# Three token blocks open the output accumulation, and VectorE takes the weight residues and the gate

## The chip, the cores and the metric

The kernel runs on one core of a Trainium2 chip. A core has TensorE (PE in the profile; its weight loads are PEld), VectorE (DVE), ScalarE (ACT), GpSimd (POOL) and SyncE (SP, which here issues all the DMAs). The metric is the device time of one execution in microseconds (us); lower is better.

## The reference, cut to what matters

One layer of sliding-window attention runs over 1024 tokens of width 2048. It has 32 query heads of size 64 and 4 key and value heads. The gate z is projected together with q, k and v.

```python
def swa_sink_mixer(h, w_in, sinks):               # h: (1, 1024, 2048)
    q, k, v, z = jnp.split(h @ w_in, [BRANCH, BRANCH + KV_A, BRANCH + 2 * KV_A], axis=-1)
...
    scores = jnp.einsum('bnqhgd,bnkhd->bnhgqk', q, kb) * (HEAD_DIM ** -0.5)
    scores = scores - slopes[:, :, None, None] * dist
    scores = jnp.where(valid[None, :, None, None], scores, NEG)
    p = jax.nn.softmax(jnp.concatenate([scores, sink_col], axis=-1), axis=-1)[..., :-1]
    o = jnp.einsum('bnhgqk,bnkhd->bnqhgd', p, vb).reshape(B, S, BRANCH)
    return o, z

    h = rmsnorm(x, g_pre)
    y = (o * jax.nn.silu(z)) @ w_out
    x = x + rmsnorm(y, g_post)
```

All inputs and outputs are float32.

## The kernel before, in words

**Products.** Every large matrix product is made in three passes. An operand is split into a part rounded for the matmul ("hi") and what is left of it ("lo"), and a product is hi·hi + lo·hi + hi·lo. A weight granule is 128x512. ACT casts its hi part (`g_hi`, L209), an elementwise engine subtracts to get its lo part (`g_lo`, L213), SP stores the lo part in DRAM (`lo`, L215), and in the second half it is loaded from there instead of made again. Of the granules of the input projection, those with `key[2] == 1` have their subtraction on GpSimd, 32 in all; the other subtractions are on VectorE.

**Stages.** The tokens go in two halves of 512. In each half come v, k, then eight quads of heads (`in_phase`), each of 16 slots of 12 matmuls: two accumulators for q and two for z. Between these matmuls stand those of the attention of the quad before: `s_ps` (scores), `o_ps` (values). After that the output projection runs over 16 k-tiles for each of four column chunks, with four accumulators, one for each block of 128 tokens.

**Spill.** The attention of the last quad has no further quad to stand between, so the first 13 k-tiles (`SPILL`) of output chunk 0 are spread among it. k-tile n of it is slot 128+n. Each k-tile takes 12 matmuls (`acc_o`): four token blocks, three passes. The lists `TSL_LAST` and `VSL_LAST` say in which slot the last quad's parts stand. The four accumulators of `acc_o` reuse the buffers of the last quad's `acc_i`; the fourth is freed when `z` has been read out of it (L510).

**Attention of a block.** `s_ps` is masked and gets its bias on DVE, goes through exp on ACT (`t`, L374), is scaled to `w` (L393), transposed to `wt` on DVE (L399) and rearranged to `px`. For most blocks `px` goes out to DRAM and back (`pd`, L408 and L411). For 36 blocks (those of the second half and the last quad's of the first) it is copied in 16 pieces by three engines; the string `MOVES` says which engine has which piece: A is ACT, D is DVE, P is GpSimd. Then come `f` hi (ACT, L421), `f` lo (DVE, L422), two masked selections `g` (GpSimd, L425), the value matmuls `o_ps` (L447), their copy `oc` and sum `s_o`, and the product with the gate, `u` (L463). That product is on GpSimd in the first half but for its last quad, else on VectorE. `u` is split in hi and lo for the output projection (`pump_parts`, L562 and L563), two parts ahead of their use (`LOOK_SPLIT`).

**Order.** The framework sets the order of each engine's instructions by a simulated timeline with its own costs. Matmuls are kept in the order of the program from slot 125 (`PIN_FROM`) to the end of the spill; elsewhere a ready matmul may be put ahead of one that is expected late. On one engine the instructions then run strictly in the order set.

Of the kernel before, what the change touches and what calls it, by code (L numbers as in the profile page):

```python
# [10 lines left out]
F32 = mybir.dt.float32  # L11
F32R = mybir.dt.float32r
# [4 lines left out]
ALU = mybir.AluOpType  # L17
AX = mybir.AxisListType

P = 128  # L20
# [3 lines left out]
NB = HALF // P  # L24
KC = D // P
# [10 lines left out]
NQUAD = NH // QUAD  # L36
# [7 lines left out]
LOOK_SPLIT = 2  # L44
LOOK_W = 3
# [5 lines left out]
W_BUFS = 3  # L51
PD_BUFS = 4
S_BUFS, O_BUFS = 3, 1
SPILL = 13
OUT_SLOT = 128 + SPILL
QSL, ZSL = ((4, 7), (8, 9)), (11, 15)
SSL, TSL, FSL, VSL = 8, 12, 16, (18, 15)
MOVES = "AADPAADPAADAAADP"
PRE_PARTS = (122, 124, 126)
PIN_FROM = 125  # L60
TSL_LAST, VSL_LAST = 14, ((18, 18, 18, 16), (18, 17, 16, 16))


@with_exitstack
def tile_swa_layer(
# [10 lines left out]
    nc = tc.nc  # L76
# [7 lines left out]
    hp = ctx.enter_context(tc.tile_pool(name="hp", bufs=1))  # L84
# [95 lines left out]
    wl = []  # L180
# [18 lines left out]
    def pump_split(limit):  # L199
        while state["split"] < min(limit, len(stream)):  # L200
            i = state["split"]
            pump_dma(i + 1)
            raw, lo = raws.pop(i)
            kind, key = stream[i][2:]
            if isinstance(kind, int):
                hi = wl[0][:, kind, :]
            else:
                hi = gp.tile([P, 512], F32R, tag="g_hi", name="g_hi", bufs=G_BUFS)
            nc.scalar.copy(hi, raw)  # L209
            if lo is None:  # L210
                lo = lo_tile()
                eng = nc.gpsimd if kind == "in" and key[2] == 1 else nc.vector
                eng.tensor_tensor(lo, raw, hi.bitcast(F32), op=ALU.subtract)  # L213
                kept[key] = dram.tile([P, 512], F32, name=f"lo{i}")
                nc.sync.dma_start(kept[key], lo.bitcast(F32))  # L215
            splits[i] = (hi, lo)
            state["split"] += 1

    def next_granule(look_split=LOOK_W, look_dma=LOOK_DMA):
        while isinstance(stream[state["use"]][2], int):  # L220
            state["use"] += 1
        i = state["use"]
        state["use"] += 1
        pump_split(i + 1 + look_split)
        pump_dma(i + 1 + look_dma)
        return splits.pop(i)
# [205 lines left out]
    def att_values(a, half, b):  # L432
        i = a["quad"]
        kv = i // 2
        pool = a["pool"]
        f, g = a.pop(("f", b))
        y = a["y"]
        o_ps = ps.tile([P, 4, 2, HD], F32, tag="o", name="o_ps", bufs=O_BUFS)
        flat = o_ps.rearrange("p a h i -> p (a h i)")
        for s in range(2):  # L440
            v = v_n[:, b + 1, kv, :] if s else v_s[:, b, kv, :]
            cols = slice(s * HD, (s + 1) * HD)
            terms = ((v, f[:, 0, :, cols]), (v, f[:, 1, :, cols]), (y[:, s, b, :], g[:, :, cols]))
            if half == 0 and b == 0:
                terms = terms[:2]
            for j, (lhsT, rhs) in enumerate(terms):
                ins = nc.tensor.matmul(  # L447
                    flat[:, s * 256 : (s + 1) * 256].rearrange("p (a i) -> p a i", i=HD), lhsT=lhsT, rhs=rhs,
                    start=s == 0 and j == 0, stop=j + 1 == len(terms), skip_group_check=True,
                )  # L450
                if s or j or state["pin"]:
                    tc.keep_in_program_order(ins)
        oc = pool.tile([P, 4, HD], F32, tag="oc", name="oc", bufs=1)
        s = pool.tile([P, 2, 2, HD], F32, tag="sb", name="s_o", bufs=1)
        s4 = s.rearrange("p s e i -> p (s e) i")
        nc.scalar.copy(oc[0:HD], o_ps[HD:P, :, 0, :])
        nc.scalar.copy(oc[HD:P], o_ps[0:HD, :, 1, :])
        nc.vector.tensor_tensor(s4[0:HD], o_ps[0:HD, :, 0, :], oc[0:HD], op=ALU.add)
        nc.vector.tensor_tensor(s4[HD:P], o_ps[HD:P, :, 1, :], oc[HD:P], op=ALU.add)
        sl = slice(b * P, (b + 1) * P)  # L460
        gate = nc.vector if half or i == NQUAD - 1 else nc.gpsimd
        for e in range(2):
            gate.tensor_tensor(  # L463
                a["u"][:, 2 * i + e, sl].rearrange("p (s i) -> p s i", i=HD),
                s[:, :, e, :],
                a["z", e][:, sl].rearrange("p (s i) -> p s i", i=HD),
                op=ALU.mult,
            )
# [6 lines left out]
    def run_events(slot):  # L475
        for fn in events.pop(slot, []):
            fn()
# [77 lines left out]
    def pump_parts(limit):  # L555
        while state["part"] < min(limit, len(parts)):
            i = state["part"]
            src, cols = parts[i]()
            hi = gp.tile([P, 512], F32R, tag="u_hi", name="u_hi", bufs=SPLIT_BUFS)
            lo = gp.tile([P, 512], F32R, tag="u_lo", name="u_lo", bufs=SPLIT_BUFS)  # L560
            hi_v, lo_v = (x.rearrange("p (k t) -> p k t", t=cols) if cols < 512 else x for x in (hi, lo))
            nc.scalar.copy(hi_v, src)  # L562
            nc.vector.tensor_tensor(lo_v, src, hi_v.bitcast(F32), op=ALU.subtract)  # L563
            pieces[i] = (hi, lo)
            state["part"] += 1

    def next_part():
        i = state["take"]
        state["take"] += 1
        pump_parts(i + 1 + LOOK_SPLIT)  # L570
        return pieces.pop(i)

    def out_slot(accs, k, fresh, done):
        gr = next_granule()
        u = next_part()
        for b in range(NB):
            for j, (w, uu) in enumerate(passes(gr, u)):
                mm(
                    accs[b],
                    lhsT=uu[:, b * P : (b + 1) * P],  # L580
                    rhs=w,
                    start=fresh and j == 0,
                    stop=done and j == 2,
                )

    def y_evac(acc, half, b, c, yg, gpost, junk):
        nc.scalar.activation(junk, acc, AF.Square, accum_out=ssp[:, half, b, c : c + 1])  # L587
# [49 lines left out]
    with tc.tile_pool(name="pro", bufs=1) as pro:  # L637
# [28 lines left out]
        for k in range(KC):  # L666
            if k % 2 == 0:
                gr = next_granule(1, 3)
# [29 lines left out]
    def out_accs(c):  # L698
        if c % 2 == 0:
            return [ps.tile([P, 512], F32, tag="acc", name="acc_o", bufs=4) for _ in range(NB)]  # L700
        tags = (("s", S_BUFS),) * S_BUFS + (("o", O_BUFS),) * O_BUFS
        return [ps.tile([P, 512], F32, tag=t, name="acc_s", bufs=n) for t, n in tags]
# [4 lines left out]
    with tc.tile_pool(name="att0", bufs=1) as att:  # L707
        def sq_load(b, c):
            xp = gp.tile([P, 512], F32, tag="raw", name="xp")
            nc.sync.dma_start(xp, xf[HALF + b * P : HALF + (b + 1) * P, c * 512 : (c + 1) * 512])  # L710
            at(SQ_SLOT + 6 * (4 * b + c) + 4, lambda: sq_make(xp, b, c))

        def sq_make(xp, b, c):
            xjunk = att.tile([P, 512], BF16, tag="oc", name="xjunk", bufs=1)
            tc.keep_in_program_order(nc.scalar.activation(xjunk, xp, AF.Square, accum_out=ssx1[:, b, c : c + 1]))

        for b in range(NB):
            for c in range(4):
                at(SQ_SLOT + 6 * (4 * b + c), lambda b=b, c=c: sq_load(b, c))
        at(SQ_SLOT + 6 * 16 + 4, lambda: x_scales(ssx1, rcol1))  # L720
        in_phase(0, h0, u0, att)
        accs = out_accs(0)
        for k in range(SPILL):
            run_events(128 + k)
            out_slot(accs, k, k == 0, False)
        state["pin"] = False
    h1 = (
        hp.tile([P, KC, HALF], F32R, tag="hh", name="h_hi1"),
# [2 lines left out]
    with tc.tile_pool(name="out0", bufs=1) as op:  # L731
# [26 lines left out]
        for c in range(4):  # L758
            if c:
                accs = out_accs(c)  # L760
# [13 lines left out]
    for k in range(KC):  # L774
        if k % 2 == 0:
            gr = next_granule()
# [10 lines left out]
    with tc.tile_pool(name="att1", bufs=1) as att:  # L787
        fins = {}

        def fin_start(b, c):  # L790
            fins[(b, c)] = finalize(att, b, c)

        for b in range(NB):
            at(2 * b, lambda b=b: y_scale(0, b))
            for c in range(4):
                s0 = FIN_SLOT + FIN_STEP * (4 * b + c)
                at(s0, lambda b=b, c=c: fin_start(b, c))
                at(s0 + 4, lambda b=b, c=c: fins.pop((b, c))())
        in_phase(1, h1, u1, att)
        accs = out_accs(0)  # L800
        for k in range(SPILL):
            run_events(128 + k)
            out_slot(accs, k, k == 0, False)
        state["pin"] = False
    assert not events, sorted(events)
    y01 = kvp.tile([P, 2, D], F32, tag="k", name="y01")
    yts = [y01[:, 0], y01[:, 1]] + [kvp.tile([P, D], F32, tag=t, name="y23") for t in ("vn", "vs")]
    wl += (
        hp.tile([P, KC, 512], F32R, tag="hh", name="wl_hi"),
        hp.tile([P, KC, 512], F32R, tag="hl", name="wl_lo"),  # L810
    )
    with tc.tile_pool(name="out1", bufs=1) as op:
        junk = op.tile([P, 512], BF16, name="junk2")
        for c in range(3):
# [65 lines left out]
```

## Time and profile before

| | |
|---|---|
| Median of 3 runs | 1275.71 us (1275.5 to 1277.07) |
| The profiled execution | 1278.27 us, of which the span 1276.6 us |
| PE busy | 1247.0 us, 98% of the span |
| DVE, ACT, POOL busy | 830.6, 783.2, 337.1 us (65%, 61%, 26%) |
| PE's chain of waits | 54% of the span is PE itself, 3% DMA, 1% each ACT, DVE and issue |

Times in the rows are from the span's start. A busy PE is not PE at its peak: the duration of a matmul overlaps the next one's, so the pitch from start to start is what it costs. In brackets stands the idle time ahead of an instruction and what ended it.

### The profile page before, as it was taken

Reading aid. Unit: us, or ns where it says so; the run is one execution under the profiler, and the core shown is the slowest. Engines: PE = TensorE matmul, PEld = TensorE weight load, DVE = VectorE, ACT = ScalarE, POOL = GpSimd, SP = SyncE. Lnnn points to the kernel's source line nnn. Section 1 sums busy time; section 2 is a strip of 40 time slices with the busy share of each in tenths; the row PEclk is TensorE's granted clock in tenths of the full one; section 3 lists DMA queues with packets and bytes.
Section 4 is the critical chain, followed back from the end, with each engine's and each line's share of the span. In section 5 each row is a group of like instructions: output and inputs, shape, how many; then the busy total and the mean of one; then the engine's idle time right before and its main releaser. Section 6 shows DMA issues by size and latency. Waiting matters only on the chain.

```text
span 1276.6 us, 20454 instructions
## 1 busy us (share of the span) xinstructions
PE 1247.0 (98%) x5889; PEld 1043.8 (82%) x5889; DVE 830.6 (65%) x2365; ACT 783.2 (61%) x2087; POOL 337.1 (26%) x549
## 2 busy tenths in 40 slices
PE   8989999999999989999999999999999999999997
PEld 8878888888887877888898888888888888877785
DVE  5636767667676688677732278787787777832344
ACT  4526767666666677555533377777767767854531
POOL 1332536536535532000003022242232232200000
PEclk9989999999999999999999999999999999999999
DMA  8556777767676755899886667667767676876625
GB/s 289 157 181 205 224 225 228 221 217 237 215 233 210 232 159 168 230 271 252 253 265 194 190 208 209 210 205 208 213 202 218 191 226 183 290 257 229 226 70 182
DMA packets 302576, 274.03 MB, mean 215 GB/s; under 512 B 51568, under 2 KB 213888, under 8 KB 302464
## 3 DMA queue, kind: packets, MB, share of 16 engines
q1 hardware_dynamic: 302464, 272.73, 70.0%
q8 instruction: 47, 0.77, 0.2%
q14 instruction: 65, 0.53, 0.2%
HBM read 198.21 MB, written 74.45 MB: 214 GB/s over the span
## 4 chain that ended last, share of the span: by engine, by line
PE 54%; DMA 3%; ACT 1%; issue 1%; DVE 1%; POOL 0%; DVEq 0%; POOLq 0%; ACTq 0%; SPq 0%
PE acc_i L318 28%; PE acc_o L318 10%; PE acc_s L318 7%; DMA raw<-in_w_out_a 3%; PE acc_l L843 3%; PE o_ps L447 2%; PE acc_v L617 2%; PE acc_k L318 2%; PE s_ps L318 1%; ACT u_hi L562 1%; ACT g_hi L209 0%; DVE y L855 0%; ACT junk L587 0%; DVE u_lo L563 0%; ACT wl_hi L209 0%
## 5 line engine op out<-in xcount | busy, mean ns | idle before, releaser
L318 PE MATMUL acc_i<-h_hi,g_hi 128*128 128x512 f32 x1024 | 401.3, 392 | 2.0 <-ACT g_hi L209 2.0
L318 PE MATMUL acc_i<-h_hi,g_lo 128*128 128x512 f32 x1024 | 401.0, 392 | 1.7 <-DVE g_lo L213 1.7
L318 PE MATMUL acc_i<-h_lo,g_hi 128*128 128x512 f32 x1024 | 400.7, 391 | 0.0
L209 ACT CAST g_hi<-raw 128x512 fp32r<-128x512 f32 x400 | 245.7, 614 | 123.8 <-PE acc_i L318 49.5
L318 PEld LDWEIGHTS acc_i<-h_hi,g_hi 128*128 128x128 f32 x1024 | 192.8, 188 | 41.2 <-ACT g_hi L209 2.4
L318 PEld LDWEIGHTS acc_i<-h_lo,g_hi 128*128 128x128 f32 x1024 | 193.0, 188 | 40.0
L318 PEld LDWEIGHTS acc_i<-h_hi,g_lo 128*128 128x128 f32 x1024 | 193.0, 189 | 34.0 <-DVE g_lo L213 2.0
L213 DVE TENSOR_TENSOR g_lo<-raw,g_hi 128x512 fp32r<-128x512 f32 x176 | 127.4, 724 | 62.0 <-ACT g_hi L209 60.0
L374 ACT ACTIVATE t<-t,m 128x129 f32<-128x129 f32 x256 | 102.6, 401 | 95.7 <-DVE m L364 93.9
L563 DVE TENSOR_TENSOR u_lo<-u,u_hi 128x512 fp32r<-128x512 f32 x128 | 88.9, 697 | 111.0 <-ACT u_hi L562 104.9
L425 POOL TENSOR_SCALAR_AFFINE_SELECT g<-f 64x512 fp32r<-64x512 f32 x112 | 99.8, 892 | 171.1 <-ACT f L421 135.3
L562 ACT CAST u_hi<-u 128x512 fp32r<-128x512 f32 x128 | 78.9, 618 | 84.9 <-PE acc_o L318 29.0
L405 ACT COPY px<-wt 32x128 f32<-32x128 f32 x324 | 96.3, 297 | 28.6 <-DVE wt L399 25.0
L318 PE MATMUL acc_o<-g_hi,u_hi 128*128 128x512 f32 x256 | 101.9, 398 | 4.6 <-DVE z L510 3.6
L318 PE MATMUL acc_o<-g_lo,u_hi 128*128 128x512 f32 x256 | 101.1, 395 | 0.0
L318 PE MATMUL acc_o<-g_hi,u_lo 128*128 128x512 f32 x256 | 100.5, 398 | 0.1
L364 DVE CUSTOM_DVE_ANT_0 t<-s_ps,t,nsink 128x128 f32<-128x128 f32 x256 | 87.9, 348 | 5.2
L345 POOL COPY t<-nsink 128x4 f32<-128x4 f32 x64 | 12.8, 203 | 277.4 <-DVE w L385 132.8
L144 POOL TENSOR_TENSOR rs_r<-rs_v,mhalf 128x1 f32<-128x1 f32 (+1 forms) x10 | 6.3, 645 | 297.0 <-DVE rs_v L142 297.0
L318 PE MATMUL s_ps<-k_x,q 128*128 128x320 f32 x256 | 76.6, 310 | 3.5 <-POOL q L503 3.5
L362 DVE COPY_PREDICATED s_ps<-mask,s_ps 128x64 f32<-128x64 uint32 x224 | 49.0, 223 | 46.0 <-PE s_ps L318 44.6
L422 DVE TENSOR_TENSOR f<-px,f 128x512 fp32r<-128x512 f32 x64 | 50.7, 793 | 41.6 <-ACT f L421 41.2
(150 smaller groups left out, 2179.3 us busy)
## 6 DMA issues: line engine op xcount, KB each, us to landing
raw<-in_w_in_a SPq DMA_DIRECT2D x288, 256.0 KB, 3.6
lo<-g_lo SPq DMA_DIRECT2D x208, 256.0 KB, 2.7
g_lo<-lo SPq DMA_DIRECT2D x192, 256.0 KB, 3.5
raw<-in_w_out_a SPq DMA_DIRECT2D x128, 256.0 KB, 4.0
pd<-wt SPq DMA_DIRECT2D x28, 256.0 KB, 2.2
px<-pd SPq DMA_DIRECT2D x112, 64.0 KB, 2.2
xp<-in_x SPq DMA_DIRECT2D x16, 256.0 KB, 3.9
xb<-in_x SPq DMA_DIRECT2D x64, 64.0 KB, 4.1
```

The source lines that it names most:

```text
L209: nc.scalar.copy(hi, raw)
L213: eng.tensor_tensor(lo, raw, hi.bitcast(F32), op=ALU.subtract)
L318: ins = nc.tensor.matmul(*args, **kw)
L362: nc.vector.copy_predicated(s3[:, :, P:], mask.unsqueeze(1).broadcast_to([P, 2, QTR]), s3[:, :, 0:QTR])
L364: nc.vector.tensor_tensor_reduce(out=t[:, 0:P], in0=s3[:, 0, QTR:], in1=t[:, 0:P], scale=1.0, scalar=nsink[:, i : i + 1], op0=ALU.add, op1 ...
L374: nc.scalar.activation(t, t, AF.Exp, bias=m, scale=-1.0, accum_out=den)
L405: copy(x[qrows[3 - k], c, :], wt[qrows[c], 3 - k, :])
L422: pin(nc.vector.tensor_tensor(f[:, 1], x, f[:, 0].bitcast(F32), op=ALU.subtract))
L425: nc.gpsimd.affine_select(out=g[dst].rearrange("p a (s i) -> p (a s) i", i=HD), in_=f[HD:P, l].rearrange("p a (s i) -> p (a s) i", i=HD).b ...
L562: nc.scalar.copy(hi_v, src)
L563: nc.vector.tensor_tensor(lo_v, src, hi_v.bitcast(F32), op=ALU.subtract)
L843: nc.tensor.matmul(acc, lhsT=uu[:, i * P : (i + 1) * P], rhs=w[:, k, :], start=k == 0 and j == 0, stop=k == KC - 1 and j == 2,)
```

## The change

In the spill of either half, the first two k-tiles are computed for token blocks 0 to 2, and only then for block 3. The spill has 14 k-tiles, not 13, and in the first half the values of the last block stand one slot later. In the spill the parts of `u` are split at most one ahead at first (`look`). In the first half the 32 GpSimd subtractions of weights and the GpSimd gate products are put on VectorE. In `MOVES` two of ACT's nine pieces go to GpSimd. The tile `wl` is allocated ahead of the second spill, since the longer spill looks ahead as far as its first granule.

```diff
-SPILL = 13
+SPILL = 14
...
-MOVES = "AADPAADPAADAAADP"
+MOVES = "AADPAADPAPDAPADP"
...
-TSL_LAST, VSL_LAST = 14, ((18, 18, 18, 16), (18, 17, 16, 16))
+TSL_LAST, VSL_LAST = 14, ((18, 18, 18, 17), (18, 17, 16, 16))
...
-                eng = nc.gpsimd if kind == "in" and key[2] == 1 else nc.vector
-                eng.tensor_tensor(lo, raw, hi.bitcast(F32), op=ALU.subtract)
+                nc.vector.tensor_tensor(lo, raw, hi.bitcast(F32), op=ALU.subtract)
...
-        gate = nc.vector if half or i == NQUAD - 1 else nc.gpsimd
         for e in range(2):
-            gate.tensor_tensor(
+            nc.vector.tensor_tensor(
...
+    def spill(accs):
+        run_events(128)
+        first = next_granule(LOOK_W - 1), next_part(1)
+        out_mms(accs, range(3), *first, True, False)
+        run_events(129)
+        second = next_granule(LOOK_W - 1), next_part(1)
+        out_mms(accs, range(3), *second, False, False)
+        out_mms(accs, (3,), *first, True, False)
+        out_mms(accs, (3,), *second, False, False)
+        for k in range(2, SPILL):
+            run_events(128 + k)
+            out_slot(accs, k, False, False, min(LOOK_SPLIT, 13 - k) if k < SPILL - 1 else LOOK_SPLIT)
...
         accs = out_accs(0)
-        for k in range(SPILL):
-            run_events(128 + k)
-            out_slot(accs, k, k == 0, False)
+        spill(accs)
```

The change also moves instructions on engines whose own lines it does not touch. First TensorE at the start of the first quad: `acc_i_799` is the quad's first accumulator, `acc_i_880` its second, and `g_hi_744` and `g_lo_746` are the two halves of the last granule of the first one. Before:

```order
L318 MATMUL acc_i_799<-h_hi0_128,g_hi_744 128x512
L318 MATMUL acc_i_880<-h_hi0_128,g_hi_820 128x512
L318 MATMUL acc_i_880<-h_hi0_128,g_lo_822 128x512
L318 MATMUL acc_i_880<-h_lo0_129,g_hi_820 128x512
L318 MATMUL acc_i_880<-h_hi0_128,g_hi_820 128x512
```

Now:

```order
L317 MATMUL acc_i_799<-h_hi0_128,g_hi_744 128x512
L317 MATMUL acc_i_799<-h_hi0_128,g_lo_746 128x512
L317 MATMUL acc_i_799<-h_lo0_129,g_hi_744 128x512
L317 MATMUL acc_i_799<-h_hi0_128,g_hi_744 128x512
L317 MATMUL acc_i_799<-h_hi0_128,g_lo_746 128x512
```

Before, the twelve matmuls of granule 820 stood behind the first matmul of granule 744; now the twelve of 744 stand together, and 820 comes 24 matmuls behind them. The queue of SP at the same place, before (lo17 is the store of `g_lo_746`):

```order
L215 DMA lo18_768<-g_lo_766 128x512
L191 DMA raw_806<-in_w_in_a 128x4x128
L215 DMA lo19_804<-g_lo_802 128x512
L191 DMA raw_826<-in_w_in_a 128x4x128
L215 DMA lo20_824<-g_lo_822 128x512
L191 DMA raw_846<-in_w_in_a 128x4x128
L215 DMA lo17_748<-g_lo_746 128x512
```

Now:

```order
L214 DMA lo17_748<-g_lo_746 128x512
L191 DMA raw_806<-in_w_in_a 128x4x128
L214 DMA lo18_768<-g_lo_766 128x512
L191 DMA raw_826<-in_w_in_a 128x4x128
L214 DMA lo19_804<-g_lo_802 128x512
L191 DMA raw_846<-in_w_in_a 128x4x128
```

The load of `raw_806` stood behind the store of `g_lo_766`; it now stands behind that of `g_lo_746`, which is made earlier. The third place is ACT in the first spill, where `u_hi_5890` before and `u_hi_5886` now are the same part of `u`, number 3 counted from 0 (`th` belongs to the gate z, `w` to the next block's probabilities). Before, part 2 and part 3 have these places:

```order
L562 CAST u_hi_5813<-u0_794 128x512
L374 ACTIVATE t_5770,den_5772<-t_5770,m_5771 128x129
L209 CAST g_hi_5805<-raw_5740 128x512
L393 ACTIVATE w_5844<-t_5622,rec_5842 128x3x32 x2
L393 ACTIVATE w_5844<-t_5622,rec_5842 128x32 x2
L393 ACTIVATE w_5844<-t_5622,rec_5842 128x4x32 x2
L562 CAST u_hi_5890<-u0_794 128x512
```

Now:

```order
L510 ACTIVATE th_5755<-z_5754 128x512
L373 ACTIVATE t_5622,den_5624<-t_5622,m_5623 128x129
L373 ACTIVATE t_5770,den_5772<-t_5770,m_5771 128x129
L392 ACTIVATE w_5834<-t_5622,rec_5832 128x3x32 x2
L392 ACTIVATE w_5834<-t_5622,rec_5832 128x32 x2
L392 ACTIVATE w_5834<-t_5622,rec_5832 128x4x32 x2
L373 ACTIVATE t_5770,den_5772<-t_5770,m_5771 128x129
L560 CAST u_hi_5886<-u0_794 128x512
```

The split that stood between `th` and the six `w` instructions now stands behind these and one more exp.

## Rows read from the trace of the kernel before

**Rows 1.** What PE waited for: in total, how often, the longest.

```profile
PE acc_o L318 <- DVE z L510: 3.6, 1, 3.6
PE s_ps L318 <- POOL q L503: 3.5, 3, 1.6
...
PE o_ps L447 <- POOL g L425: 1.6, 2, 1.0
PE o_ps L447 <- ACT f L421: 1.4, 1, 1.4
...
PE o_ps L447 <- DVE f L422: 1.0, 1, 1.0
```

**Rows 2.** A piece of the chain of waits in the output projection: start, length, what, how many.

```profile
521.03 43.52 PE acc_s L318 x192
```

**Rows 3.** The timeline of PE, SP, POOL and DVE in turn at the start of the first quad: start, duration, engine, line, what.

```profile
67.53 0.50 PE L318 MATMUL acc_i<-h_hi,g_hi 128*128 128x512 f32 x1 [1.99 <-ACT g_hi L209]
69.75 0.79 PE L318 MATMUL acc_i<-h_hi,g_lo 128*128 128x512 f32 x1 [1.72 <-DVE g_lo L213]
...
72.05 0.63 PE L318 MATMUL acc_i<-h_hi,g_hi 128*128 128x512 f32 x1
72.47 0.63 PE L318 MATMUL acc_i<-h_hi,g_lo 128*128 128x512 f32 x1
...
56.07 0.39 SPq L191 DMA_DIRECT2D raw<-in_w_in_a  x1
64.40 0.34 SPq L215 DMA_DIRECT2D lo<-g_lo  x1
...
59.39 1.48 POOL L213 TENSOR_TENSOR g_lo<-raw,g_hi 128x512 fp32r<-128x512 f32 x1
...
57.32 0.69 DVE L301 TENSOR_TENSOR k<-acc_k,rrow 128x512 f32<-128x512 f32 x1 [1.71 <-ACT rrow L264]
```

**Rows 4.** Three stretches at a lower clock: stretch, its length, PE, PEld, DVE, ACT and POOL busy (instructions), the clock granted to PE as a share of full speed, DMA share, GB/s.

```profile
68.20:74.90 6.70, 5.15 (x12) 4.09 (x13) 1.85 (x4) 0.05 (x1) 0.00 (x0) 0.50 0.64 193
467.60:470.90 3.30, 3.30 (x10) 2.62 (x9) 3.29 (x12) 2.75 (x10) 0.00 (x0) 0.50 0.52 141
505.10:511.80 6.70, 6.06 (x16) 4.80 (x17) 2.68 (x7) 1.35 (x3) 1.05 (x1) 0.50 0.51 172
```

**Rows 5.** The timeline at the start of the first spill: PE, DVE, ACT, and DVE again.

```profile
466.91 0.50 PE L318 MATMUL acc_o<-g_hi,u_hi 128*128 128x512 f32 x1 [3.64 <-DVE z L510]
...
466.16 0.69 DVE L510 TENSOR_TENSOR z<-acc_i,rrow 128x512 f32<-128x512 f32 x1
...
469.97 1.65 ACT L393 ACTIVATE w<-t,rec 128x96 f32<-128x96 f32 x6
...
471.65 0.71 DVE L399 STREAM_TRANSPOSE wt<-w 128x512 f32<-128x512 f32 x1 [0.59 <-ACT w L393]
```

**Rows 6.** The timeline at the end of the first spill: ACT, DVE, POOL, PE.

```profile
499.36 2.77 ACT L405 COPY px<-wt 32x128 f32<-32x128 f32 x9
...
503.20 0.61 ACT L421 CAST f<-px 128x512 fp32r<-128x512 f32 x1
...
509.58 0.62 ACT L562 CAST u_hi<-u 128x512 fp32r<-128x512 f32 x1 [1.25 <-DVE u L463]
...
498.86 1.11 DVE L405 COPY px<-wt 32x128 f32<-32x128 f32 x4
...
504.01 1.14 DVE L422 TENSOR_TENSOR f<-px,f 128x512 fp32r<-128x512 f32 x1
505.07 0.68 DVE L213 TENSOR_TENSOR g_lo<-raw,g_hi 128x512 fp32r<-128x512 f32 x1
...
503.88 0.74 POOL L425 TENSOR_SCALAR_AFFINE_SELECT g<-f 64x512 fp32r<-64x512 f32 x1 [4.21 <-ACT f L421]
505.22 1.05 POOL L425 TENSOR_SCALAR_AFFINE_SELECT g<-f 64x512 fp32r<-64x512 f32 x1 [0.61 <-DVE f L422]
...
506.33 0.58 PE L447 MATMUL o_ps<-g,v_y 128*128 128x256 f32 x1 [0.54 <-POOL g L425]
```

**Rows 7.** The timeline ahead of the longest wait of `s_ps`, at 395 us: ACT, SP, POOL.

```profile
391.72 0.62 ACT L421 CAST f<-px 128x512 fp32r<-128x512 f32 x1 [2.41 <-DMA px<-pd]
...
388.30 1.74 SPq L411 DMA_DIRECT2D px<-pd  x4
...
392.47 1.12 POOL L425 TENSOR_SCALAR_AFFINE_SELECT g<-f 64x512 fp32r<-64x512 f32 x1 [3.94 <-issue]
```

**Rows 8.** Groups of instructions: busy time, mean ns of one, idle time before. The first is of the stretch 62 to 461 us (the first half's quads), the second and third of the whole run, the last of 652 to 1085 us (the second half up to its spill).

```profile
L213 DVE TENSOR_TENSOR g_lo<-raw,g_hi 128x512 fp32r<-128x512 f32 x97 | 73.2, 754 | 47.3 <-ACT g_hi L209 45.6 <-DMA lo<-g_lo 1.2
...
L213 POOL TENSOR_TENSOR g_lo<-raw,g_hi 128x512 fp32r<-128x512 f32 x32 | 41.5, 1298 | 29.9 <-ACT g_hi L209 14.4 <-DMA raw<-in_w_in_a 12.2 <-DMA lo<-g_lo 2.0
...
L463 POOL TENSOR_TENSOR u<-s_o,z 128x128 f32<-128x128 f32 x56 | 25.2, 471 | 45.7 <-DVE s_o L459 45.7
...
L463 DVE TENSOR_TENSOR u<-s_o,z 128x128 f32<-128x128 f32 x56 | 16.5, 335 | 0.3
```

**Rows 9.** Busy time by stretch, columns as in rows 4: a stretch of the first half's quads, the second half's quads, its spill.

```profile
280.00:330.00 50.00, 48.99 (x232) 41.04 (x231) 36.92 (x111) 34.82 (x104) 31.36 (x41) 1.00 0.75 228
...
697.00:1085.00 388.00, 388.00 (x1824) 325.40 (x1823) 285.86 (x983) 274.39 (x797) 98.58 (x196) 1.00 0.69 205
1085.00:1121.00 36.00, 36.00 (x172) 30.22 (x171) 28.65 (x90) 28.76 (x78) 8.43 (x16) 1.00 0.84 287
```

More of the change, by code (lines that the diff above doesn't have):

```diff
@@ L565, in pump_parts, with next_part, out_mms @@
             state["part"] += 1
-    def next_part():
+    def next_part(look=LOOK_SPLIT):
         i = state["take"]
         state["take"] += 1
-        pump_parts(i + 1 + LOOK_SPLIT)
+        pump_parts(i + 1 + look)
         return pieces.pop(i)
[L573 to L576, printed above, removed]
+    def out_mms(accs, blocks, gr, u, fresh, done):
+        for b in blocks:
             for j, (w, uu) in enumerate(passes(gr, u)):
@@ L584, in out_slot @@
                 )
+    def out_slot(accs, k, fresh, done, look=LOOK_SPLIT):
+        out_mms(accs, range(NB), next_granule(), next_part(look), fresh, done)
+    def spill(accs):
[10 more added lines that the diff above has]
+            out_slot(accs, k, False, False, min(LOOK_SPLIT, 13 - k) if k < SPILL - 1 else LOOK_SPLIT)
     def y_evac(acc, half, b, c, yg, gpost, junk):
@@ L799, in tile_swa_layer @@
         in_phase(1, h1, u1, att)
+        wl += (
+            hp.tile([P, KC, 512], F32R, tag="hh", name="wl_hi"),
+            hp.tile([P, KC, 512], F32R, tag="hl", name="wl_lo"),
+        )
         accs = out_accs(0)
-        for k in range(SPILL):
-            run_events(128 + k)
-            out_slot(accs, k, k == 0, False)
+        spill(accs)
         state["pin"] = False
@@ L807, in tile_swa_layer @@
     yts = [y01[:, 0], y01[:, 1]] + [kvp.tile([P, D], F32, tag=t, name="y23") for t in ("vn", "vs")]
[L808 to L811, printed above, removed]
     with tc.tile_pool(name="out1", bufs=1) as op:
```

## The prediction

> **What bounds the kernel now.** I read the page first (the table above): PE is busy nearly all the time, so a gain can only come from the places where PE stands still or runs at the low clock. The list of PE's waits comes next [rows 1]: the reader is to see that they are few and single, a wait for z, three for q, some around `o_ps`. What a matmul costs at full speed is read from the output projection: 43.52 us for 192 is 0.227 us each [rows 2]. Then the granted clock by stretch [rows 4]: at three places it is 0.50, the lower level of 1.2 GHz, and each lies right behind a wait. There a matmul costs 72.47 - 72.05 = 0.42 us [rows 3], so a wait is paid for twice. Four places remain:
>
> - A, start of the first quad. PE stops at 67.53 - 1.99 = 65.54 and the low clock ends at 74.90 [rows 3, 4]. In these 9.36 us run 13 matmuls (the one at 67.53 and the twelve of rows 4's first line), worth 13 x 0.227 = 2.95. Lost: 6.4 us.
> - B, start of the spill. 3.64 idle for z [rows 5], then 3.30 us at the low clock, of which 1 - 0.227/0.42 = 46% is lost, 1.5 [rows 4]. Lost: 5.1.
> - C, the last block's values. 1.4 for f hi, 1.0 for f lo, 0.54 for g [rows 1, 6], then 6.06 busy us at the low clock, 46% of it 2.8 [rows 4]. Lost: 5.7.
> - D, inside the first half's quads: 3.5 for q and a part of the 1.6 for g [rows 1], some 4.5 us; the clock is 1.00 in the stretch of [rows 9] that has 1.0 of it.
>
> **The change part by part.**
>
> *Weight subtractions, at A.* The POOL subtraction of 59.39 was over at 60.87, long before PE wanted it [rows 3]. PE waits because of the order: it takes granule 820 ahead of 746's residue, and 820 is late, since SP's queue had its load behind the store lo18, and nothing was issued from 56.07 until 64.40 [rows 3]. In the new order PE keeps to granule 744, whose residue DVE makes right behind the k read-out (57.32 + 0.69 = 58.0, then about 0.75 by the mean of [rows 8]): 58.8 against a want at 65.5. The load behind lo17 leaves some 5 us earlier than 64.40. Granule 820 is now wanted behind 744's twelve matmuls and 24 more, at 65.5 + 36 x 0.227 = 73.7, while before it was there by 69.75 with its load late. The granules between hang on DVE's k work, whose last residue before came in time for 69.75. I see nothing late: **-6.4**. The bounds are -6.4 and 0 (the wait goes to one of the granules between).
>
> *Weight subtractions and gates, at D.* DVE gets 32 x 0.754 = 24.1 and 56 x 0.335 = 18.8 us [rows 8], 42.9 us over the 399 us of the first half's quads, 5.4 in 50; its fullest stretch goes from 36.92 to 42.3 of 50, 85% [rows 9]. PE does not wait for DVE there, but for q and g of POOL. POOL itself was idle 3.94 before g: f came late on ACT, which waited for the px loads, issued at 388.30 [rows 7]. So a lighter POOL does not take these waits away, and a fuller DVE moves that chain (w, transposition, f, q) back a little. In the second half DVE is at 285.86 of 388, 74%, with the gates on it, and PE is busy through all 388 [rows 9]. Bounds: -2 (the POOL pieces in the chain, 0.47 and 1.30 each, no longer in the way at some of four places) and +4 (each of the four longer by a subtraction and a gate, about 1 us). I take **+0.5**, near no change, since the order on ACT and POOL around f, g and q stays.
>
> *Block order, at B.* Nine more matmuls stand ahead of the fourth block: PE gets to it at 466.91 - 3.64 + 9 x 0.227 = 465.3. z, ahead of which DVE waits for ACT's copies, starts about when it did: two ACT copies less, 2 x 2.77/9 = 0.6 earlier [rows 6], and two gates more, 2 x 0.335 = 0.7 later [rows 8]. So PE waits until 467, 1.7 instead of 3.64: -1.9. A stretch of the quads with 50.00 - 48.99 = 1.0 us idle kept the clock at 1.00 [rows 9], while 3.64 in one piece lost it, so I take the low clock as gone too, though 1.7 lies between: -1.5. Against it stands part 3 of u. Its split is asked for later, and on ACT it now stands behind the six w and one more exp. With the two instructions gone that stood before w (0.6 each, a cast of u and a cast of a granule), w starts at 468.8 to 469.5 in place of 469.97 [rows 5], the hi part is there after 1.65 + 0.4 + 0.6, at 471.5 to 472.2, and the lo part behind the transposition, 0.71 [rows 5], and four copies, 1.1 [rows 6], at about 473.5. PE wants them 18 matmuls (4.1) and two scores (0.3) behind 467, at 471.4, the lo part 0.5 later. A new wait of about 1.7, and the low clock after it in a third of cases, 0.5. Sum **-1.2**; bounds -5.1 (no wait left) and +1.7 (the new wait 3.4, with the low clock).
>
> *One more k-tile, at C.* Twelve matmuls, 2.7 us, stand ahead of the values, out of what came behind. The f cast at 503.20 stood behind nine copies, a cast of u and one of a granule [rows 6]; two copies (0.6) and the granule's cast (0.6) are out of its way. The three waits come to 2.9 us, and the k-tile and the shorter chain take 2.7 + 1.2 off, which would leave nothing; but the chain goes on through DVE and POOL, and an earlier PE start (A, B) does not bring it forward. I leave 1.1 of a wait with the clock up: **-4.6**; bounds -5.7 and -2 (1.5 of wait, and half of the low clock stays). Behind the values only twelve matmuls, 2.7 us, now cover the path to the next part of u: its hi part ended at 510.20, 3.9 behind the last release of PE at 506.33 [rows 6], of which four value matmuls at half clock took about 1.2. That leaves 2.7 against 2.7, and the first matmuls use only the hi part, so it holds by a hair.
>
> POOL and DVE hinder each other there. The f subtraction beside POOL's selection took 1.14, beginning 0.13 behind it; the second selection took 1.05 where the first had 0.74, beside a subtraction of a granule begun at 505.07 [rows 6]. In the Trainium skill, "SBUF — State Buffer", section "Who interferes with whom", a VectorE instruction with two SBUF inputs and a GpSimd instruction that reads SBUF shut each other out for the whole of one of them; the trace agrees (503.88 + 0.74 = 504.62, and the subtraction ends 0.53 later). In the new order no granule's subtraction stands ahead of f's, which would then start first and hold POOL: by the rule the second selection ends some 0.4 earlier, and C would be -5.0. I leave it out of the sum.
>
> *MOVES and wl.* In the second spill PE waits for nothing, 36.00 busy of 36 [rows 9], and ACT has 7.2 us idle there. Nothing to gain; two more POOL copies cost little beside POOL's 8.43 of 36: 0, bounds -1 and +2.
>
> Sum: -6.4 + 0.5 - 1.2 - 4.6 = -11.7 us. The profiled execution took 1278.27, so it would be 1266.6; the median of the runs is 2.56 lower, and I put the same sum on it: 1275.71 - 11.7 = **1264.0 us**.
>
> **The rivals.**
>
> 1. *All spill waits go.* z starts earlier than I put it and part 3 is in time. For it: DVE loses waits of ACT there. Against it: the order behind w. -6.4 - 5.1 - 5.7 = -17.2, 1258.5.
> 2. *The waits move.* Part 3 stops PE as long as z did, with the low clock, and C keeps half of its own: B 0, C -2.8, -6.4 + 0.5 - 2.8 = -8.7, 1267.0. For it: the clock fell at all three places where waits came together [rows 4].
> 3. *VectorE becomes the bound in the first half, and the kernel is slower.* Each of the 28 blocks there has a chain with a DRAM round trip, and at four or more of them it is already on the edge [rows 1, 7]. A subtraction (0.75) and half a pair of gates (0.33) ahead of w's transposition or of f move it by 1.1 us. If half the blocks show it, 14 x 1.1 = 15.4 us is more than A to C give (12.2): 1279. It decides from 12.2 / 14 = 0.87 us a block. Against it: PE waits nowhere for DVE there, and the second half runs without a wait. In the Trainium skill, "Perfetto Trace Analysis", section "Optimizing Scalar/DVE Operations", work may go from a saturated VectorE to other engines, even GpSimd; the change goes the other way, but no stretch shows DVE saturated (85% by the sum above).
> 4. *The order is not what decides at A*: the wait stays, behind another granule, -5.3, 1270.4.
>
> **How the numbers follow.** The forecast has 0.52 (its own range 1261 to 1267), rival 1 0.14, rival 2 0.19, rival 4 0.09, rival 3 0.06. About 0.2% (2.6 us) can be told from no change. Faster by more than that are all but rival 3 and a tenth of rivals 2 and 4 with D at its upper bound: 0.90; same 0.05; slower 0.05. The range goes from 1256 (rival 1 with some of D) to 1271 (rival 4).
>
> **What would show it.** Right: no wait of `acc_i` in the first 30 us of the first quad and a clock of 1.00 there; a wait for z below 2 us; a wait of `acc_o` for u_hi or u_lo in the k-tile behind it; a short wait at the values with the clock up. Wrong: SP still silent from 56 to 64 us; new waits of `acc_i`, `s_ps` or `o_ps` for DVE between 100 and 460 us; the low clock behind part 3.

## The result, and the profile after

| | before | changed |
|---|---|---|
| median | 1275.61 us (1274.31 to 1277.07, 4 runs) | 1265.49 us (1264.41 to 1266.23, 4 runs) |
| ratio to before | | 0.992, 95% interval 0.9903 to 0.9937 |
| profiled execution, span | 1278.27, 1276.6 us | 1265.93, 1264.2 us |

The forecast was 1264.0 us, 11.7 less; measured are 10.1 less. To see where they come from, I take for every matmul the distance to the next one's start, less the pitch of its size at full clock (0.227 us for 512 columns, 0.146 for 320, 0.117 for 256), and sum what is left by place. This counts waits and low clock together.

| lost, us | prologue | A | D | B | C | second half | its end | sum |
|---|---|---|---|---|---|---|---|---|
| before | 7.3 | 6.7 | 8.0 | 5.7 | 6.6 | 3.3 | 4.9 | 42.5 |
| changed | 5.6 | 0.1 | 8.8 | 5.4 | 1.6 | 3.5 | 5.2 | 30.2 |

The sums differ by 12.3 us, as do the spans (12.4). I do not put the prologue's 1.7 us down to the change: over the profiles below it lies between 4.5 and 6.0 us whatever the kernel. In this pair of profiles the gain is A and C, 11.6 us; B and D give nothing.

The list of PE's waits of the changed kernel, its head, as in [rows 1]:

```profile
PE o_ps L446 <- POOL g L424: 3.9, 5, 1.3
PE s_ps L317 <- DVE m L363: 2.2, 1, 2.2
...
PE acc_o L317 <- DVE u_lo L561: 0.9, 1, 0.9
...
PE s_ps L317 <- POOL q L501: 0.7, 2, 0.4
PE o_ps L446 <- DVE f L421: 0.5, 2, 0.3
```

The wait for z, longest before, is gone from the list. A wait for m stands in its place, a new one for u_lo has come, and what was a wait for q is now one for g. Two stretches by windows (columns as in [rows 4]): the first quad's start, and the one low-clock stretch that is left.

```profile
458.60:462.00 3.40, 3.40 (x9) 2.64 (x8) 3.37 (x10) 1.15 (x3) 0.00 (x0) 0.50 0.43 130
62.40:80.00 17.60, 17.60 (x79) 14.59 (x78) 11.16 (x17) 5.68 (x10) 5.31 (x6) 1.00 0.69 217
```

At A, PE is busy throughout with the clock at 1.00. The other rows at A, of SP and DVE, against [rows 3]:

```profile
57.41 0.39 SPq L191 DMA_DIRECT2D raw<-in_w_in_a  x1
62.93 0.34 SPq L214 DMA_DIRECT2D lo<-g_lo  x1
...
68.87 0.69 DVE L212 TENSOR_TENSOR g_lo<-raw,g_hi 128x512 fp32r<-128x512 f32 x1
```

SP is still silent for 5.5 us, and the lo half of granule 820 (the last row) is done at 69.56. Before it was made here (ACT, DVE):

```profile
65.58 1.26 ACT L308 CAST k_x<-k 64x512 fp32r<-64x512 f32 x2 [2.28 <-DVE k L301]
66.86 0.62 ACT L209 CAST g_hi<-raw 128x512 fp32r<-128x512 f32 x1
...
69.00 0.69 DVE L213 TENSOR_TENSOR g_lo<-raw,g_hi 128x512 fp32r<-128x512 f32 x1
```

So it was done at 69.69 then, behind a prologue that was 1.7 us longer: it came no earlier with the change, but TensorE asked for it later. What made 820 late before was no transfer. Its cast on ACT stood behind two casts of k, and these waited for DVE's k. B in the timeline: ACT, DVE, PE.

```profile
454.01 2.15 ACT L404 COPY px<-wt 32x128 f32<-32x128 f32 x7
456.18 0.62 ACT L209 CAST g_hi<-raw 128x512 fp32r<-128x512 f32 x1
...
456.83 0.69 DVE L212 TENSOR_TENSOR g_lo<-raw,g_hi 128x512 fp32r<-128x512 f32 x1 [0.63 <-ACT g_hi L209]
457.44 0.35 DVE L363 CUSTOM_DVE_ANT_0 t<-s_ps,t,nsink 128x128 f32<-128x128 f32 x1
...
459.99 0.68 DVE L508 TENSOR_TENSOR z<-acc_i,rrow 128x512 f32<-128x512 f32 x1
...
467.47 0.68 DVE L561 TENSOR_TENSOR u_lo<-u,u_hi 128x512 fp32r<-128x512 f32 x1
...
453.54 0.39 PE L317 MATMUL acc_o<-g_hi,u_hi 128*128 128x512 f32 x1
...
457.94 0.39 PE L317 MATMUL s_ps<-k_x,q 128*128 128x320 f32 x1 [2.18 <-DVE m L363]
...
468.21 0.50 PE L317 MATMUL acc_o<-g_hi,u_lo 128*128 128x512 f32 x1 [0.90 <-DVE u_lo L561]
```

The score matmul behind the first nine `acc_o` matmuls needs the buffer that the maximum m frees. On DVE m stands behind a granule's subtraction, and that waits for its cast on ACT, which stands behind seven px copies. The read-out of z ends 7.1 us behind the first `acc_o` matmul (453.54). C, against [rows 6]: DVE, POOL, PE.

```profile
496.11 0.94 DVE L461 TENSOR_TENSOR u<-s_o,z 128x128 f32<-128x128 f32 x2
496.98 0.68 DVE L421 TENSOR_TENSOR f<-px,f 128x512 fp32r<-128x512 f32 x1
...
501.32 0.49 DVE L461 TENSOR_TENSOR u<-s_o,z 128x128 f32<-128x128 f32 x2
...
495.81 0.90 POOL L424 TENSOR_SCALAR_AFFINE_SELECT g<-f 64x512 fp32r<-64x512 f32 x1 [2.65 <-ACT f L420]
497.72 1.05 POOL L424 TENSOR_SCALAR_AFFINE_SELECT g<-f 64x512 fp32r<-64x512 f32 x1 [1.01 <-DVE f L421]
...
497.71 0.38 PE L446 MATMUL o_ps<-f,v_s 128*128 128x256 f32 x1 [0.20 <-DVE f L421]
498.83 0.39 PE L446 MATMUL o_ps<-g,v_y 128*128 128x256 f32 x1 [0.73 <-POOL g L424]
```

PE waits 0.9 us there instead of 2.9, and the clock stays up.

### The profile page after: what moved, and what is told of

Its sections match the earlier page's. It is cut to its first block, busy times and chain, and to the rows that moved or that the text cites. A ratio compares the mean times of both kernels' runs of the same rounds, so it can differ in the third digit from the quotient of the medians.

```text
span 1264.2 us, 20400 instructions
## 1 busy us (share of the span) xinstructions
PE 1241.9 (98%) x5889; PEld 1039.6 (82%) x5889; DVE 861.2 (68%) x2453; ACT 764.8 (60%) x2015; POOL 290.2 (23%) x533
## 4 chain that ended last, share of the span: by engine, by line
PE 55%; DMA 4%; ACT 2%; issue 1%; DVE 1%; POOL 0%; SPq 0%; DVEq 0%; POOLq 0%; ACTq 0%
PE acc_i L317 28%; PE acc_o L317 11%; PE acc_s L317 7%; DMA raw<-in_w_out_a 4%; PE acc_l L851 3%; PE o_ps L446 2%; PE acc_v L629 2%; PE acc_k L317 2%; PE s_ps L317 2%; ACT u_hi L560 1%; ACT g_hi L209 1%; DMA lo<-g_lo 0%; ACT wl_hi L209 0%; DVE y L863 0%; DVE u_lo L561 0%
## 5 line engine op out<-in xcount | busy, mean ns | idle before, releaser
L212 DVE TENSOR_TENSOR g_lo<-raw,g_hi 128x512 fp32r<-128x512 f32 x208 | 152.5, 734 | 47.3 <-ACT g_hi L209 42.4
L404 ACT COPY px<-wt 32x128 f32<-32x128 f32 x252 | 74.9, 297 | 17.6 <-DVE wt L398 14.5
L317 PE MATMUL acc_s<-g_hi,u_hi 128*128 128x512 f32 x192 | 74.8, 390 | 0.9 <-ACT u_hi L560 0.9
L362 DVE SCALAR_TENSOR_TENSOR t<-distb,s_ps 128x128 f32<-128x128 f32 x256 | 71.2, 284 | 5.3
```

Source lines behind the costliest of these rows:

```text
L212: nc.vector.tensor_tensor(lo, raw, hi.bitcast(F32), op=ALU.subtract)
L317: ins = nc.tensor.matmul(*args, **kw)
L362: nc.vector.scalar_tensor_tensor(t[:, 0:P], distb, 2.0 ** -i, s3[:, 1, QTR:], op0=ALU.mult, op1=ALU.add)
L404: copy(x[qrows[3 - k], c, :], wt[qrows[c], 3 - k, :])
```

## The experiments

The theory: each stall is a matter of what stands ahead of what on one engine; A hangs on one granule, C on the lead of the f chain, and more work on VectorE only costs. The main rival: VectorE's speed is what helps, and the gain is spread over the 88 moved instructions. The runs were made on four other chips; each ratio is against before on the same chip, whose medians were 1270.6 to 1274.4 us. Single executions of one kernel lie up to 7.5 us from their median there, so intervals tell more than medians. The columns A to C are us lost in each run's profile, counted as above.

| run | ratio, 95% interval | A | D | B | C |
|---|---|---|---|---|---|
| e1_subs | 1.0008, 0.9988 to 1.0028 | 0.1 | 6.8 | 8.3 | 5.3 |
| e10_subs_again | 1.0027, 1.0011 to 1.0043 | 0.1 | 11.2 | 8.4 | 6.9 |
| e9_onesub_before | 0.9946, 0.9929 to 0.9964 | 0.1 | 6.4 | 5.7 | 6.9 |
| e2_gates | 0.9972, 0.9957 to 0.9988 | 6.5 | 8.7 | 4.8 | 1.2 |
| e3_blocks | 0.9952, 0.9931 to 0.9973 | 5.9 | 5.7 | 4.2 | 1.7 |
| e4_ktile | 0.9965, 0.9950 to 0.9981 | 5.9 | 8.7 | 7.1 | 1.3 |
| a0_after | 0.9948, 0.9929 to 0.9967 | 0.1 | 8.0 | 5.4 | 1.6 |
| e5_moves | 0.9950, 0.9934 to 0.9967 | 0.1 | 9.3 | 5.4 | 2.1 |
| e7_onesub | 0.9931, 0.9904 to 0.9957 | 0.1 | 9.3 | 3.2 | 1.7 |
| e8_poolgates | 0.9949, 0.9934 to 0.9963 | 0.1 | 9.4 | 4.7 | 0.1 |
| f3_lolate | 0.9918, 0.9894 to 0.9942 | 0.1 | 6.1 | 1.9 | 3.0 |
| f4_poolgates | 0.9901, 0.9877 to 0.9924 | 0.1 | 8.0 | 1.4 | 1.3 |

**The changed kernel again (a0_after).** It ran unchanged on the chip of e5, e7 and e9. Expected were about 0.992 of before, and 0.995 or more if the gain depends on the chip. It took 1262.83 us against 1271.39, 0.9948. The interval leaves out 0.992, though it overlaps that of the first chip. On this chip the whole change can't be told from one subtraction alone (e9_onesub_before, 0.9946), although its profile lost 5.3 us less in C. The profile of e9_onesub_before was the longest of its twelve executions, 2.7 us above their median. So the 11.6 us of A and C are what a pair of profiles shows, and not a gain that the times of every chip bear out.

**The subtractions alone (e1_subs, e10_subs_again).** The kernel before with the change's one line:

```diff
-                eng = nc.gpsimd if kind == "in" and key[2] == 1 else nc.vector
-                eng.tensor_tensor(lo, raw, hi.bitcast(F32), op=ALU.subtract)
+                nc.vector.tensor_tensor(lo, raw, hi.bitcast(F32), op=ALU.subtract)
```

> The kernel before with the 32 weight subtractions on VectorE alone. Theory (the stall at the first quad comes from where TensorE and the DMA queue stood in the order, and goes with the subtractions): no wait of acc_i between 62 and 80 us, clock 1.00 there, spill as before; 6.5 us less than before, and at most 1 us given back in the first half's quads, so about 1270. Rival (part of the gain needs the gates or the block order too): 1272 or more, with an acc_i wait left. Rival (a fuller VectorE costs more than 3 us in the quads): 1273 or more with the acc_i wait gone.

> The kernel before with all 32 subtractions on VectorE a second time, since it timed like before although its profile had no wait at the first quad. Theory (a fuller VectorE gives the gain back in waits that vary from run to run): again 0.998 to 1.003 of before, the z wait near 4.8 us with the low clock, and more lost in the quads than the 6.8 us of the first profile. Rival (the first timing was off): 0.993 to 0.996, as with one subtraction.

A was gone in both profiles, 6.6 us, and yet neither timing was below before; the second is above it. The waits of the second run show where the time went:

```profile
PE o_ps L446 <- POOL g L424: 6.2, 5, 2.0
PE acc_o L317 <- DVE z L509: 4.8, 1, 4.8
...
PE s_ps L317 <- POOL q L502: 1.7, 1, 1.7
```

z held PE 1.2 us longer than in [rows 1], with a longer low clock behind it (B 8.4 for 5.7), and PE waited 6.2 us in all for g, not 1.6. D varies between the two profiles, 6.8 and 11.2; the first was of the fastest of its twelve executions (3.7 us below their median), the second 1.9 above its median. So the other 31 subtractions give A's gain back.

That a fuller VectorE does it is not shown. In the 20 us ahead of the spill VectorE is no busier in e10_subs_again than with one subtraction (the third busy time is its; e10_subs_again, then e9_onesub_before):

```profile
437.02:457.02 20.00, 19.58 (x96) 16.38 (x94) 14.61 (x45) 12.79 (x38) 10.37 (x16) 1.00 0.58 180
...
431.29:451.29 20.00, 20.00 (x99) 16.95 (x97) 14.82 (x46) 13.95 (x42) 11.99 (x18) 1.00 0.62 196
```

Its row there waits for f of the last DRAM round trip ahead of the spill, and that comes late. SP and ACT in e10_subs_again, then in the kernel before:

```profile
441.61 0.41 SPq L214 DMA_DIRECT2D lo<-g_lo  x1
442.24 1.79 SPq L410 DMA_DIRECT2D px<-pd  x4
447.50 0.62 ACT L420 CAST f<-px 128x512 fp32r<-128x512 f32 x1 [1.87 <-DMA px<-pd]
...
446.21 1.74 SPq L411 DMA_DIRECT2D px<-pd  x4
450.37 0.62 ACT L421 CAST f<-px 128x512 fp32r<-128x512 f32 x1 [1.15 <-DMA px<-pd]
```

The last subtraction that GpSimd had ends sooner on VectorE, 15.6 us ahead of the spill and not 14.1, and the store of its lo part now stands right ahead of the px loads. f begins 5.3 us behind the issue of these loads, 4.2 in the kernel before. In all six profiles with the 32 subtractions on VectorE that store stands there (5.0 to 5.7 us), in none of the other eight (3.4 to 4.6). No run moves the store alone, so this is a reading and not a test.

**One subtraction (e9_onesub_before).** Granule 746 has number 17 in the stream of granules:

```diff
-                eng = nc.gpsimd if kind == "in" and key[2] == 1 else nc.vector
+                eng = nc.gpsimd if kind == "in" and key[2] == 1 and i != 17 else nc.vector
```

> The kernel before with the subtraction of granule 746 alone on VectorE. Theory (the first quad's stall is one granule's place in the order, and all 32 subtractions on VectorE gave the gain back in the other stages): no acc_i wait at 62 to 80 us, clock 1.00 there, spill as before, 5 to 7 us less than before. Rival (time gained at the first quad is lost again in later waits whatever the subtractions cost, as with all 32): within 1.5 us of before.

The theory holds: 0.9946, some 7 us, with one instruction on another engine. TensorE's order at the first quad became that of the changed kernel, z's wait stayed:

```profile
PE acc_o L318 <- DVE z L510: 3.6, 1, 3.6
```

**The gates alone (e2_gates).** The change's edit of `gate`, on the kernel before.

> The kernel before with the gate products on VectorE alone. Theory (the waits for q and g in the first half hang on a DRAM round trip and change little): within 1.5 us of before, the acc_i wait at 65 to 70 us still there. If the gates are what moved the waits from q to g: q waits below 1 us and g waits above 3 us in all, sum unchanged.

The time fell by more than I expected, and not for the reason that I gave. q waits stayed at 2.6 us, so the gates did not move the waits from q to g. C fell from 6.6 to 1.2, because f is cast earlier in ACT's row, before TensorE asks for it. What TensorE waits for now is the sum `s_o` of the block before (ACT, PE):

```profile
492.07 1.65 ACT L393 ACTIVATE w<-t,rec 128x96 f32<-128x96 f32 x6
...
498.62 0.61 ACT L421 CAST f<-px 128x512 fp32r<-128x512 f32 x1
499.26 0.37 ACT L456 COPY oc<-o_ps 64x256 f32<-64x256 f32 x1
...
494.35 0.40 PE L447 MATMUL o_ps<-f,v_s 128*128 128x256 f32 x2
...
501.49 0.48 PE L447 MATMUL o_ps<-f,v_s 128*128 128x256 f32 x2 [0.81 <-DVE s_o L459]
```

In the kernel before the same two rows stand so (ACT, PE):

```profile
496.63 0.90 ACT L393 ACTIVATE w<-t,rec 128x32 f32<-128x32 f32 x3
...
496.11 0.40 PE L447 MATMUL o_ps<-f,v_s 128*128 128x256 f32 x2
```

Measured from the first value matmul of the block before, f begins 4.3 us behind it (498.62 and 494.35), in the kernel before 7.1 (503.20 and 496.11). Of these 2.8 us, 2.0 are w, which ends 0.6 ahead of that matmul and not 1.4 behind it; the rest is the two `oc` copies, which now stand behind f.

**The block order alone (e3_blocks).** `spill` as in the diff above, with `SPILL` 13 and the other values as before.

> The kernel before with the block order of the spill alone (13 k-tiles, last values in the old slot, MOVES as before). On VectorE the maximum m of the waiting score block stands ahead of the granule's subtraction here, behind it in the changed kernel. Theory (the new 2.2 us wait of s_ps for m comes from that VectorE order, not from the block order): no wait of s_ps above 0.5 us at the spill's start, a z wait of 1 to 2 us, clock 1.00, and about 1 us for part 3 of u: 2 to 4 us less than before. Rival (the block order itself brings the score matmul three matmuls forward to where m is late): s_ps waits about 2 us again with the clock at 0.50, and less than 1 us is gained.

```profile
PE acc_o L318 <- DVE z L510: 2.0, 1, 2.0
...
PE o_ps L447 <- DVE s_o L459: 1.3, 1, 1.3
PE acc_o L318 <- DVE u_lo L563: 1.2, 1, 1.2
```

No s_ps wait, z 2.0, no stretch of low clock at the spill's start, part 3 of u 1.2: the forecast's picture of B, with this edit alone. B fell by 1.5. The rest of the gain, to 0.9952, is mostly C (6.6 to 1.7), where w and f moved up in ACT's row as with the gates: f begins 4.8 us behind that matmul.

**The k-tile alone (e4_ktile).** `SPILL` 14 and the last values one slot later, the old loop with `look` as in the change.

> The kernel before with 14 k-tiles and the last values one slot later, block order and MOVES as before. Theory (the k-tile alone covers the f chain): waits at the last values 1.0 to 1.6 us in all, clock 1.00 there, 4 to 5.5 us less than before. Rival (the two copies moved off ScalarE are needed too): waits of 2 us or more at the last values, clock down, 3 us or less gained.

C fell by 5.3 us, as forecast, without the copies taken off ScalarE. ACT's row is that of before here (f begins 7.1 us behind the value matmul), but 36 matmuls of `acc_o` stand between the values, not 24: this is the lead of a k-tile. B was 1.4 higher in this profile, with a longer low clock behind the same z wait (3.8 us); the ratio, 0.9965, is some 4.5 us.

**MOVES back (e5_moves).** The changed kernel with one line undone:

```diff
-MOVES = "AADPAADPAPDAPADP"
+MOVES = "AADPAADPAADAAADP"
```

> The changed kernel with MOVES as before (nine px copies on ScalarE, three on GpSimd). On VectorE the maximum m of the score block stands ahead of the granule's subtraction again. Theory (the 2.2 us wait of s_ps for m comes from MOVES, through that order): no s_ps wait above 0.5 us at the spill's start, in its place a z wait of 1 to 2 us, clock 1.00 there; 1 to 3 us less than the changed kernel. Rival (the wait only changes its name): a z wait of 3 us or more with the clock at 0.50, and no gain against the changed kernel.

The order of m and the subtraction turned as expected, the wait for m fell to 0.6, and z took its place:

```profile
PE acc_o L317 <- DVE z L508: 2.2, 1, 2.2
...
PE s_ps L317 <- DVE m L363: 0.6, 1, 0.6
```

B is 5.4 as with the new MOVES, the clock falls again, and the time is the same: 0.9950 and 0.9948. My rival held but for the size of the wait (2.2, not 3 or more): the order of these two decides only which wait bears VectorE's lateness.

**31 subtractions back on GpSimd (e7_onesub).** The changed kernel with the line of e9_onesub_before.

> The changed kernel with 31 of the 32 weight subtractions back on GpSimd; only the one of granule 746 (the last of the first quad's first accumulator) is on VectorE. Theory (that one granule sets the order at the first quad, and the other 31 only load VectorE): no acc_i wait at 62 to 80 us, and 1 to 6 us less than the changed kernel, as the waits for q and g in the quads shrink. Rival (the 31 are needed, GpSimd being the late one in the quads): q and g waits grow, 1 us or more above the changed kernel.

B fell from 5.4 to 3.2 with the clock at 1.00 throughout the spill; no wait for m is left there, 0.3 for z and 1.5 for u_lo. A stayed away. D did not shrink (9.3), against my expectation. The time is 1.0 us lower by the medians, which the intervals cannot tell from nothing.

**The gates back on GpSimd (e8_poolgates).** The changed kernel with the `gate` lines of before.

> The changed kernel with the gate products of the first half back on GpSimd. Theory (the gates on VectorE neither help nor harm by more than 1.5 us; they only decide whether the late round trip shows at q or at g): within 1.5 us of the changed kernel (0.992 to 0.996 of before), q waits above 2 us again and g waits below 3. Rival (the gates on VectorE bought part of the gain, as the gates alone on the kernel before took 3.7 us off): 0.997 of before or more, with the waits at the last values longer than 2 us.

The ratio is that of the changed kernel, 0.9949 to 0.9948. The waits for q did not come back (none in the quads, g 3.1), so here too the gates are not what moved q to g.

**Late lo (f3_lolate), and only one subtraction returned (f4_poolgates).** In the spills' k-tile 3 the four u_lo matmuls go behind the eight that need u_hi only; the first run is on e7_onesub, the second has the gates on GpSimd as well.

```diff
-        for b in blocks:
-            for j, (w, uu) in enumerate(passes(gr, u)):
+        steps = [(b, j) for b in blocks for j in range(3)]
+        if late_lo:
+            steps.sort(key=lambda bj: bj[1] == 2)
+        for b, j in steps:
+            for w, uu in passes(gr, u)[j : j + 1]:
```

> The version with 31 subtractions on GpSimd, and in the spills' fourth k-tile (number 3) the eight matmuls that need only u hi are put ahead of the four that need u lo. Theory (TensorE waits there for part 3's lo half alone, 1.5 us): the wait of acc_o for u_lo at the spill's start goes, at most 0.5 us for u_hi stays; the spill's start loses about 1.6 us (3.2 before it), and the time is 1 to 1.7 us below the version with 31 subtractions on GpSimd, about 0.992 of before. Rival (the hi half is as late, the lo half only the last of the two): u_hi waits 1 us or more in its place and less than 0.5 us is gained.

> The late-lo version with the first half's gate products back on GpSimd too, so that of all the work returned to VectorE only one subtraction (granule 746) is left; block order, 14 k-tiles and MOVES stay. Theory (the gain of the change comes from the order at the first quad and from the spill; the engine that carries the other subtractions and the gates gives nothing): 0.989 to 0.994 of before, no acc_i wait at the first quad, no z or m wait above 1 us at the spill's start. Rival (the gates on VectorE carry part of the gain): 0.995 or more, with more than 9 us lost in the first half's quads.

The u_lo wait is gone and B is 1.9, then 1.4. In f3_lolate a wait of 1.2 for f lo came up at the last values, and C rose to 3.0; I had not forecast it. The start of the spill in the second run, by windows:

```profile
450.00:470.00 20.00, 19.88 (x89) 15.57 (x88) 17.02 (x54) 16.92 (x50) 6.71 (x15) 1.00 0.43 135
```

PE is idle for 0.12 us there, with the clock at 1.00. f4_poolgates took 1261.22 us against 1274.38 on its chip, 0.9901. It has of all the work returned to VectorE one subtraction, so 87 of the 88 returned instructions are not needed for the gain. (It has the late lo beside that; e7_onesub and e8_poolgates, without it, show the same for the 31 and the 56 by themselves.) Whether it beats the changed kernel is not settled: its interval ends at 0.9924, the changed kernel's two begin at 0.9903 and 0.9929, and they were not run on one chip.

## Why the prediction was right, and where it was not

**A, forecast -6.4: measured -6.6.** The size was right, and that the order decides; rival 4 fell. The step on the queue of SP was wrong. Granule 820 comes from `raw_770`, which left at 56.07, ahead of the store lo18, so it was not held up there. SP is silent after the change too, and 820's residue comes no earlier. The load behind lo17 did leave early, at 57.41, but it is `raw_806`, for granule 840. What made 820 late was ACT's row, where its cast stood behind two casts of k that waited for DVE (65.58 and 66.86). TensorE takes it 35 matmuls later in its row, and with that the stall is gone (e9_onesub_before). One granule was enough. It is the second of its accumulator's four granules, not the last, as I had called it: the 24 matmuls between are those of the third and fourth.

**B, forecast -1.2: measured -0.3.** The step that failed is "PE waits until 467, 1.7 instead of 3.64 ... I take the low clock as gone too". z was in time, because PE had stopped 2.18 us earlier for m and then lost the clock. I had not followed the score matmul, which the block order puts behind nine matmuls in place of twelve, nor what stands ahead of m on VectorE. The step "z ... starts about when it did" failed too: z ended 7.1 us behind the first `acc_o` matmul, before 5.8 (466.16 + 0.69, and 461.06), so that with m in time PE still waits for z (e5_moves, 2.2). The rival "the waits move" described B in size, with another wait than the one I named. The edit alone did what I forecast (e3_blocks: z 2.0, clock up); with the 32 subtractions z comes later, and B is 2.2 us worse than without 31 of them (e7_onesub, where z ends 4.9 us behind that matmul). Part 3 of u was mis-sized at 1.7 with a share of low clock: 0.9 of wait, clock up. The first `acc_o` matmul of before:

```profile
461.06 0.39 PE L318 MATMUL acc_o<-g_hi,u_hi 128*128 128x512 f32 x1
```

**C, forecast -4.6: measured -5.0.** The term was right, and so was that the k-tile suffices (e4_ktile). That it was needed is not so: block order or gates alone clear most of C, since w and f stand earlier in ACT's row. The sentence on the port of VectorE and GpSimd gave 0.4 us more if f's subtraction went first. It did not: the u split and the gates stand ahead of it, it began at 496.98, 1.2 behind the selection, and the second selection took 1.05 again. That the two hinder each other shows in the gates: a pair took 0.94 beside a selection and 0.49 alone. Leaving the 0.4 out was right.

**D, forecast +0.5: measured +0.8** in one profile and 0.0 in the other, no more than two runs of one kernel differ (6.8 and 11.2). In three profiles D also holds a stretch of low clock, behind a wait for g of 2.3 to 2.7 us (e1_subs, e4_ktile, e8_poolgates). The waits changed from q to g, which I had not forecast. Neither gates alone (q 2.6) nor gates taken back (q none) explain it. The subtractions alone show g waits of 2.9 and 5.5 us in the quads, but without 31 of them the changed kernel still has 3.3. What decides it stays open.

**Rival 3, VectorE as the bound.** I gave it 0.06 for the whole change. Its price was there on the kernel before: the other 31 subtractions cost all that A gave and some more (8 and 10 us, from 0.9946 with one of them to 1.0008 and 1.0027 with all). I had priced them, with the gates, at 0.5. That VectorE is the bound is not shown, as the 20 us ahead of the spill say; the chain with the round trip came later, as this rival has it, but perhaps by the store in SP's queue. In the changed kernel the same subtractions cost 2.2 us of B in the profiles, and 1.0 us by the medians (e7_onesub), which can't be told from nothing; why so little there stays open. So the total came out right with one term (A) for a partly wrong reason, one (B) too good by 0.9, and one (C) as forecast. That it came so near 11.7 is in part luck: the same kernel took 8.6 us off by the medians on the second chip.

**Two bounds** do not follow from what I gave for them: the upper one of B comes to +1.5, not +1.7 (-1.9 - 1.5 + 3.4 + 1.5), and that of C to -2.8, not -2 (5.7 less 1.5 and 1.4). Neither is in the sum.

**MOVES, forecast 0**: 0.9950 without and 0.9948 with it.

## What to carry to other kernels

When a stall lies behind an order, look for the one instruction whose expected time made the order, and move that one; in the kernel before, moving its 31 fellows with it gave the whole gain back. When work is put ahead of a wait, follow every matmul that moves forward with it, not only the one that waited. And before calling an edit the cause, run it alone: here three different edits cleared the same stall at C, two by an earlier place of f on ScalarE and one by the lead of a k-tile.

## What was not expected of the hardware

The low clock does not follow from the length of one wait. At the spill's start a wait of 2.0 us for z kept the clock at 1.00 (e3_blocks), and one of 2.2 for z lost it (e5_moves, with 0.6 for m ahead of it). In the quads a wait of 2.3 for g kept it (f4_poolgates), and one of the same length lost it (e4_ktile). The two waits, each with the stretch behind it, f4_poolgates first:

```profile
226.78 0.39 PE L447 MATMUL o_ps<-g,v_y 128*128 128x256 f32 x1 [2.34 <-POOL g L425]
226.70:232.00 5.30, 5.22 (x26) 4.45 (x27) 3.63 (x12) 3.94 (x14) 1.51 (x3) 1.00 0.77 240
...
231.43 0.48 PE L447 MATMUL o_ps<-g,v_y 128*128 128x256 f32 x1 [2.31 <-POOL g L425]
...
231.60:234.90 3.30, 3.30 (x11) 2.82 (x12) 2.06 (x8) 2.58 (x10) 1.47 (x2) 0.50 0.67 223
```

By the rates of [rows 4] I estimate that a spill start without the low clock (3.3 us, 46% of it lost) is worth 1.5 us more than its waits say. The second thing is how far single executions differ: two profiles of one kernel lost 6.8 and 11.2 us in the first half's quads, so one profile cannot tell a change of 2 us there.
